# An encoder kernel on one core: moving the X, B and C projections ahead of the chunked scan as seven-product pairs

## The chip, the cores and the metric

The kernel runs on one core of a Trainium2 chip. The metric is the device time of one execution in microseconds (us). Engines are named as in the profile: PE (TensorE) with its weight loads PEld, DVE (VectorE), ACT (ScalarE), POOL (GpSimd) and SP (SyncE), which issues the transfers.

## What is computed

Two encoder layers run over 1024 tokens of width 1024. Only the first, the even one, is touched:

```python
proj = x @ w_in
z, xbc, dt_raw, sc_bg, sc_cg, sc_h, sc_gate = _split(proj, EVEN_SIZES)
xbc = jax.nn.silu(_depthwise_conv(xbc, conv_w, SSD_CONV_PAD) + conv_b)
xs, bm, cm = _split(xbc, (SSD_INNER, SSD_GROUPS * SSD_STATE, SSD_GROUPS * SSD_STATE))
y_a = _ssd_bidirectional(
...
y_a = _rms_norm(y_a.reshape(b, S, SSD_INNER).astype(x.dtype) * jax.nn.silu(z), norm_g)
y_b = sc_bg * _depthwise_conv(sc_cg * sc_h, sc_conv_w, (1, 1)) * jax.nn.silu(sc_gate)
return jnp.concatenate([y_a, y_b], axis=-1) @ w_out
```

So `x @ w_in` gives, in blocks of 128 channels, 8 blocks of X, 4 of B, 4 of C (each with a four-tap convolution over the tokens and a SiLU) and 4 x 8 blocks of the gated short convolution ("gate blocks"), beside z and dt. The scan (SSD) works on four groups of heads; a group g needs X blocks 2g and 2g+1, B block g and C block g.

## The kernel before, in words

All matmuls keep float32 accuracy by splitting each operand into a high and a low part (`split`, L481: ACT makes the high part, L483, and DVE or POOL the low one, L484) and multiplying three times (`mm3`, `mm6`, L401 to L412). The four tiles of x (high and low) stay in SBUF all through the first layer. They sit in the pool `big` of eight buffers of 2 MB; the other four serve in turn.

**A full block** (`op_fm`, L657) is one block of 128 output channels against all of x: eight steps kk of six matmuls of 512 columns into a PSUM tile `gps`. `fm_finish` (L617) then takes it out: for X, B and C a convolution and a SiLU by halves (`conv_half`, L585: an Identity on ACT, three scalar_tensor_tensor on DVE at L593, a Tanh on ACT, one more on DVE at L598) into the group's tile `xfm`; for gate blocks (`br_conv`, L603, and L637 to L653) products with a three-tap convolution, stored to DRAM as `ybd`.

**A pair** (`op_sp`, L891, with its weight sums in `op_sw`, L835) makes two blocks at once from 2 x 2 blocks by Winograd's scheme: seven block products of twelve matmuls of 512 columns each, where two full blocks would take eight. It needs four tiles of sums of x, `xT4` (`op_tp`, L821, also from `big`: two loads `xtraw` into the weight buffers `wraw`, four differences on DVE at L827, two splits). The raw weights of a pair (`sraw`, L841) use the same three `wraw` buffers. Pairs are used for the gate blocks j = 4 to 7: eight pairs, all behind the SSD.

**The SSD** per group: `op_p2` and `op_p2s` (L697, L717) for eight chunks: transposes of xfm into `xps`, scaling by DVE (L712), a split with POOL, the chunk's state `sps`; `op_z` (L677) adds the z projection of the chunk for groups 1 to 3 (24 matmuls of 256 columns); `op_p2b` (L745) ends the state recurrence. Then `op_p3f` and `op_p3b` (L756, L776) for eight chunks: a 512 KB row broadcast `E` loaded from DRAM, a mask added by DVE (L768; held behind the sixth chunk's L712 by an order edge), eight exponentials on ACT (L771), products on PE (`cbp`, `yo`, `yd`), sums on DVE and POOL, a gate on POOL (L798) and a store. A group's `xfm`, `zx` and `hin` come from `big`, so with the next group's xfm all eight buffers are taken.

**Order.** `main_plan` (L78) lists all steps: steps of full blocks stand in a queue and are pulled between the SSD's (F2 per chunk in the first half of a group, F3 in the second). Here they are the X, B, C blocks of group 0 (before the SSD) and of groups 1 to 3, and the gate blocks j = 0 to 3; 16 steps are left and run behind the SSD, beside `op_end`, the last two `op_tp` and the first pair's weight sums. The list is not the order of issue: the program is built with a scheduler that plans on a timeline, takes on each engine the earliest listed instruction that is ready in its plan, and gives buffers out of a pool as they are freed. `issue_after` adds an order edge. Weights come through `Weights` (L250): loads into three `wraw` buffers, splits into three `whi` and three `wlo`.

## Time and profile before

| | |
|---|---|
| median of 3 runs | 1423.87 us (1423.72 to 1426.09) |
| time of the profiled execution | 1426.95 us |
| its span in the profile | 1424.8 us |
| mean granted TensorE clock | 0.997 of full speed |
| start until the first full block, 0 to 35 us | PE busy 28.28 us |
| full blocks, z and SSD | 35 to 555 us |
| eight pairs behind the SSD, with the end of the first layer's gating | 555 to 727 us |
| output projection, second layer | 727 to 1425 us |

A line of the timeline or of the chain gives start, duration, engine, line of the kernel, operation, output tile <- inputs, shapes and count; in brackets the idle time ahead of it and who ended it. [...] Busy times of PE overlap: a matmul of 512 columns counts as 0.39 us, but the next starts 0.23 us after it.

### The profile page before, as it was taken

The numbers are of one execution on the slowest core, as the hardware profiler recorded it, in microseconds if no ns is written. First come the engines' busy times: TensorE is split into PE (matmuls) and PEld (weight loads), VectorE is DVE, ScalarE is ACT, GpSimd is POOL, SyncE is SP. The second block draws the span as 40 slices with busy tenths as digits, with TensorE's granted clock in tenths as the row PEclk, the third lists the DMA queues.
The fourth block names the chain that finished last, engine by engine and source line by source line (L and its number), as shares of the span: only waits on it lengthen the run. The fifth ranks groups of instructions, "written<-read, shape, count | busy, mean of one in ns | idle before, by whom it ended". The sixth has DMA issues, their size and how long they took to land.

```text
span 1424.8 us, 19565 instructions
## 1 busy us (share of the span) xinstructions
PE 1394.6 (98%) x7287; PEld 1187.2 (83%) x7287; DVE 931.3 (65%) x1512; ACT 655.7 (46%) x1301; POOL 478.7 (34%) x443
## 2 busy tenths in 40 slices
PE   8999999999999999999999999999999999999997
PEld 8887798888889787788888888898888888988886
DVE  5758858839965947866564543733327888888485
ACT  5446545537536423433243422522225888878410
POOL 0013635423733543433210430612310445546210
PEclk9999999999999999999999999999999999999999
DMA  7221523421430524232268355211100000001232
GB/s 253 69 72 45 119 75 91 109 82 32 144 114 10 150 82 140 80 95 74 85 196 274 104 159 192 81 32 45 44 23 1 1 1 1 1 31 60 89 118 89
DMA packets 47726, 123.39 MB, mean 87 GB/s; under 512 B 5512, under 2 KB 10384, under 8 KB 47632
## 3 DMA queue, kind: packets, MB, share of 16 engines
q1 hardware_dynamic: 47632, 122.14, 27.8%
q8 instruction: 58, 0.95, 0.3%
q14 instruction: 36, 0.29, 0.1%
HBM read 105.21 MB, written 16.91 MB: 86 GB/s over the span
## 4 chain that ended last, share of the span: by engine, by line
PE 79%; DVE 10%; DMA 3%; ACT 3%; issue 2%; POOL 2%; DVEq 0%; SPq 0%; ACTq 0%; POOLq 0%
PE sA L907 6%; PE gps L409 5%; PE gps L410 5%; PE gps L412 5%; PE ops L412 4%; PE ops L410 4%; PE ops L409 4%; PE tps L1390 3%; PE fps L404 3%; PE fps L402 3%; PE fps L403 3%; PE sD L907 3%; PE sps L402 2%; PE sps L403 2%; PE sps L404 2%
## 5 line engine op out<-in xcount | busy, mean ns | idle before, releaser
L409 PE MATMUL gps<-x,whi 128*128 128x512 f32 x512 | 206.2, 403 | 3.6 <-DVE cacc L593 3.0
L410 PE MATMUL gps<-x,whi 128*128 128x512 f32 x512 | 202.3, 395 | 0.0
L412 PE MATMUL gps<-x,wlo 128*128 128x512 f32 x512 | 162.8, 396 | 0.1
L484 DVE TENSOR_TENSOR wlo<-wraw,whi 128x1024 fp32r<-128x1024 f32 x66 | 85.4, 1297 | 76.7 <-ACT whi L483 76.5
L483 ACT CAST whi<-wraw 128x1024 fp32r<-128x1024 f32 x66 | 69.0, 1049 | 122.7 <-PE ops L412 38.6
L409 PEld LDWEIGHTS gps<-x,whi 128*128 128x128 f32 x512 | 96.7, 189 | 26.4 <-issue 3.1
L412 PEld LDWEIGHTS gps<-x,wlo 128*128 128x128 f32 x512 | 95.7, 189 | 21.2 <-issue 1.2
L410 PEld LDWEIGHTS gps<-x,whi 128*128 128x128 f32 x512 | 96.7, 189 | 19.7 <-issue 1.2
L1376 POOL TENSOR_SCALAR pt<-pt,sm 128x1024 f32<-128x1024 f32 x64 | 72.8, 1138 | 114.3 <-DVE sm L1375 63.3
L484 POOL TENSOR_TENSOR xdl<-xd,xdh 128x512 fp32r<-128x512 f32 (+1 forms) x32 | 40.2, 1256 | 178.7 <-ACT xdh L483 175.3
L484 DVE TENSOR_TENSOR PT<-tps,PT 128x512 fp32r<-128x512 f32 x128 | 84.1, 682 | 14.2 <-ACT PT L483 14.0
L771 ACT ACTIVATE E<-E,eb 128x128 f32<-128x128 f32 x256 | 78.4, 391 | 25.3 <-DVE E L768 17.9
L1370 DVE TENSOR_REDUCE nm<-sps 128x1 f32<-128x1024 f32 x64 | 77.9, 1218 | 9.5 <-PE sps L404 9.3
L987 POOL TENSOR_TENSOR rs<-rs,neghalf 128x1 f32<-128x1 f32 x16 | 12.9, 811 | 210.5 <-DVE nm L1022 142.8
L1374 ACT ACTIVATE pt<-sps,nm 128x1024 f32<-128x1024 f32 x64 | 71.8, 1122 | 17.4 <-DVE nm L1371 12.6
L483 ACT CAST PT<-tps 128x512 fp32r<-128x512 f32 x128 | 70.0, 588 | 17.2 <-PE tps L1390 16.6
L795 POOL TENSOR_TENSOR ta<-to,ta 128x256 f32<-128x256 f32 x56 | 57.5, 1027 | 53.0 <-DVE to L788 50.1
L402 PE MATMUL fps<-x1hi,whi 128*128 128x512 f32 x192 | 74.9, 390 | 0.0
L404 PE MATMUL fps<-x1hi,wlo 128*128 128x512 f32 x192 | 74.7, 389 | 0.0
L403 PE MATMUL fps<-x1lo,whi 128*128 128x512 f32 x192 | 74.7, 389 | 0.0
L593 DVE SCALAR_TENSOR_TENSOR cacc<-gps,vec,cacc 128x512 f32<-128x512 f32 (+1 forms) x96 | 71.5, 745 | 2.4 <-ACT cacc L589 1.4
L1390 PE MATMUL tps<-consts,pt 128*128 128x128 f32 x512 | 70.9, 274 | 0.6 <-DVE PT L484 0.3
(372 smaller groups left out, 3823.9 us busy)
## 6 DMA issues: line engine op xcount, KB each, us to landing
wraw<-in_wt_dram SPq DMA_DIRECT2D x82, 512.0 KB, 4.3
E<-crow SPq DMA_DIRECT2D x32, 512.0 KB, 5.6
sraw<-in_wt_dram SPq DMA_DIRECT2D x16, 512.0 KB, 4.3
yad<-yg SPq DMA_DIRECT2D x32, 128.0 KB, 2.2
ybd<-bra SPq DMA_DIRECT2D x16, 256.0 KB, 2.4
xtraw<-in_xT_dram SPq DMA_DIRECT2D x8, 512.0 KB, 3.8
yab<-yad SPq DMA_DIRECT2D x8, 512.0 KB, 3.5
ybr<-ybd SPq DMA_DIRECT2D x8, 512.0 KB, 4.4
```

The source lines that it names most:

```text
L402: nc.tensor.matmul(out, shi, mhi, start=start, stop=False)
L403: nc.tensor.matmul(out, shi, mlo, start=False, stop=False)
L404: nc.tensor.matmul(out, slo, mhi, start=False, stop=stop)
L409: nc.tensor.matmul(out, shi, mhi, start=start, stop=False)
L410: nc.tensor.matmul(out, shi, mlo, start=False, stop=False)
L412: nc.tensor.matmul(out, slo, mhi, start=False, stop=stop)
L483: nc.scalar.copy(out=hi, in_=src)
L484: lo_eng.tensor_tensor(out=lo, in0=src, in1=hi.bitcast(F32), op=ALU.subtract)
L771: A.activation(out=E4[:, d, h], in_=E4[:, d, h], func=AF.Exp, bias=eb4[:, c, d, 4 * g + h:4 * g + h + 1])
L907: PE.matmul(ps, s_[:, kk, :], x_, start=fresh and kk == 0 and m == 0, stop=kk == 3 and m == 2, skip_group_check=True)
L1370: V.tensor_reduce(out=nm, in_=ps, axis=AX.X, op=ALU.max)
L1390: PE.transpose(out=ps[:, P * c:P * c + P], in_=pt[:, P * (4 * h + c):P * (4 * h + c) + P], identity=k.ident)
```

## The change

- The first block of gates, j = 0, is computed as full blocks right after the z and dt projection. The four `op_tp` run beside it.
- X, B and C of all groups then run as eight pairs (one pair of B and C and one of X per group). Their convolution is on whole rows of 1024 out of SBUF (`conv_silu`), with a Silu on ACT in place of Tanh and a DVE multiplication, and the result goes to DRAM (`xbd`, 512 KB a block). Each group loads its 2 MB `xfm` back (`op_xl`), group 0 before the SSD, the next ones at the end of the first half of the group before.
- group 0's z goes to DRAM and back (`z0d`). The decay tables (`dt_chain`) are made ahead of the pairs, with buffers of the front pool `fp`.
- In the SSD the only full blocks are gates j = 1 to 4, 128 steps: 16 before group 0, 2 with each chunk of its first half, 3 with each chunk of every second half. In the second halves a block's first step has an order edge behind the group's last transpose (`op_hold`).
- The `big` tiles of the sums are given up for the SSD, so `op_tp` runs again as before: two in the last group's second half, two behind it. The queue of full blocks is empty by then.
- Six gate pairs (j = 5 to 7) stay behind the SSD.
- In the front pairs all three split weights of a pair take the three `whi`/`wlo` buffers; behind the SSD the third has buffers of its own, as before.

```diff
-F2, F3, FB, FC = 0, 6, 4, 0
-J0 = 4
+F2, F3, FB, FX = (2, 0, 0, 0), 3, 0, 16
+JF, J0 = 1, 5
...
-    def to_front(keys):
-        n = 0
-        while n < len(queue) and queue[n][2] != 0:
-            n += 1
-        queue[n:n] = [s for key in keys for s in tile_steps(key)]
-
...
-    for key in (("B", 0), ("C", 0), ("X", 0), ("X", 1)):
-        queue += tile_steps(key)
-    ops.append(("dt",))
-    pull(len(queue))
-    for j in range(J0):
+    def pairs(first, count, sched, final):
+        for n in range(first, first + count):
+            for i in range(7):
+                ops.append(("sp", n, i))
+                if n + 1 < first + count:
+                    ops.extend(("sw", n + 1, m) for m in sched.get(i, ()))
+            if n + 2 < first + count:
+                ops.append(("sw", n + 2, 0))
+            ops.extend(final.get(n, ()))
+
+    for j in range(JF):
         for q in BR_ORDER:
             queue += tile_steps(("br", q, j))
+    ops.append(("zx",))
+    per = len(queue) // 4
+    for t in range(4):
+        pull(per // 2)
+        ops.append(("tp", t))
+        if t == 3:
+            ops.append(("sw", 0, 0))
+        pull(per - per // 2)
+    pull(len(queue))
+    ops += [("sw", 0, i) for i in range(1, SW_N)]
+    ops.append(("sw", 1, 0))
+    ops.append(("dt",))
+    pairs(0, NF, SW_FRONT, {})
+    for j in range(JF, J0):
+        for q in BR_ORDER:
+            queue += tile_steps(("br", q, j))
+    ops.append(("ssd",))
+    pull(FX)
     for g in range(G):
         ops.append(("z0", g))
         pull(FB)
...
-            pull(F2)
+            pull(F2[g])
...
         if g + 1 < G:
-            to_front([("X", 2 * g + 2), ("X", 2 * g + 3), ("B", g + 1), ("C", g + 1)])
+            ops.append(("xl", g + 1))
+        ops.append(("hold", g))
         ops.append(("p3f", g, C3[0]))
-        pull(FC)
...
             pull(F3)
             ops.append(("p3b", g, c))
-        while any(s[1][0] in ("B", "C", "X") for s in queue):
-            pull(1)
+        ops.append(("hold", None))
...
-    ops += [("sw", 0, i) for i in range(SW_N)]
+    ops += [("sw", NF, i) for i in range(SW_N)]
     pull(len(queue))
-    ops.append(("sw", 1, 0))
-    for n in range(NP):
-        for i in range(7):
-            ops.append(("sp", n, i))
-            if n + 1 < NP and 0 < i + 1 < SW_N:
-                ops.append(("sw", n + 1, i + 1))
-        if n + 2 < NP:
-            ops.append(("sw", n + 2, 0))
-        if n in YA_P:
-            ops.append(("ya", YA_P.index(n)))
+    ops.append(("sw", NF + 1, 0))
+    pairs(NF, NP - NF, SW_BACK, {NF + n: [("ya", i)] for i, n in enumerate(YA_P)})
...
+SW_FRONT = {1: (1,), 3: (2,), 5: (3, 4), 6: (5,)}
+SW_BACK = {i: (i + 1,) for i in range(5)}
 SW_N = 6
 YA_P = (1, 2)
-PAIRS = [p for j in range(J0, 8) for p in ((("br", 1, j), ("br", 2, j)), (("br", 3, j), ("br", 0, j)))]
+PAIRS = [p for g in range(G) for p in ((("B", g), ("C", g)), (("X", 2 * g), ("X", 2 * g + 1)))]
+NF = len(PAIRS)
+PAIRS += [p for j in range(J0, 8) for p in ((("br", 1, j), ("br", 2, j)), (("br", 3, j), ("br", 0, j)))]
 NP = len(PAIRS)
...
-        self.limit = self.seq.index(("O", 0))
+        self.limits = [4 * JF, self.seq.index(("O", 0)), len(self.seq)]
+        self.limit = self.limits.pop(0)
...
     def release(self):
-        self.limit = len(self.seq)
-        self.split(self.used + 1 + self.ahead)
+        self.limit = self.limits.pop(0)
+        self.split(self.used + 1)
...
+    k.xbd = k.dram.tile([G, P, 4, S], F32, name="xbd")
+    k.z0d = k.dram.tile([P, NB, 256], F32, name="z0d")
...
+    def op_zx():
+        nonlocal fp
...
+            zs = view(dtp.tile([P, 512], F32, name="z0", tag="z0", bufs=2)[:, 0:256 * n], n)
...
+            nc.sync.dma_start(out=k.z0d[:, c:c + n], in_=zs)
...
+    def acc4(name):
+        return fp.tile([P, S], F32, name=name, tag="acc", bufs=2)
+
+    def op_dt():
+        tm = [view(acc4("dtmp"), 4) for _ in range(2)]
+        dt_chain(k, [t[:, i] for t in tm for i in range(4)], t4("rowT"), dtx)
+
+    def op_ssd():
+        nonlocal fp, cvp, tp, eb4, dw4, ecs4, et4
+        fctx.close()
+        fp = None
+        cvp = bctx.enter_context(tc.tile_pool(name="cvp", bufs=1))
+        tp = sctx.enter_context(tc.tile_pool(name="ssdt", bufs=1, side="right"))
         eb4, dw4, ecs4, et4 = (t.rearrange("p (c d h) -> p c d h", c=NB, d=2) for t in (k.eb, k.dw, k.ecs, k.etot))
+        op_xl(0)
+
+    def op_xl(g):
+        groups[g]["xfm"] = view(big(k, "xfm").bitcast(F32), 4)
+        for j in (2, 3, 0, 1):
+            nc.sync.dma_start(out=groups[g]["xfm"][:, j], in_=k.xbd[g, :, j])
 
...
+    def conv_silu(key, u):
+        kd = key[0]
+        g, j = (key[1] // 2, key[1] % 2) if kd == "X" else (key[1], 2 + "BC".index(kd))
+        idx = key[1] if kd == "X" else 8 + 4 * (j - 2) + g
+        w = lambda i: k.vec[:, V_CONVW + 4 * idx + i:V_CONVW + 4 * idx + i + 1]
+        acc = acc4("cacc")
+        A.activation(out=acc, in_=u, func=AF.Identity, bias=k.vec[:, V_CONVB + idx:V_CONVB + idx + 1], scale=w(2))
+        for i, sh in ((1, -1), (0, -2), (3, 1)):
+            a0, a1 = max(-sh, 0), S - max(sh, 0)
+            V.scalar_tensor_tensor(out=acc[:, a0:a1], in0=u[:, a0 + sh:a1 + sh], scalar=w(i), in1=acc[:, a0:a1], op0=ALU.mult, op1=ALU.add)
+        A.activation(out=acc, in_=acc, func=AF.Silu)
+        nc.sync.dma_start(out=k.xbd[g, :, j], in_=acc)
...
+    hold = None
+
+    def op_hold(g):
+        nonlocal hold
+        hold = None if g is None else groups[g]["xp"]
 
     def op_fm(key, kk):
         if kk == 0:
             live[key] = (W.get(key), k.pa.tile([P, 1024], F32, name="gps", tag="pa"))
         (whi, wlo), ps = live[key]
         wh, wl = view(whi, KD), view(wlo, KD)
-        mm6(nc, halves(ps), wh[:, kk, :], wl[:, kk, :], *zip(*(xhl(h, kk) for h in range(2))), kk == 0, kk == KD - 1)
+        with tc.issue_after(hold) if hold is not None and kk == 0 else nullcontext():
+            mm6(nc, halves(ps), wh[:, kk, :], wl[:, kk, :], *zip(*(xhl(h, kk) for h in range(2))), kk == 0, kk == KD - 1)
...
     def op_z0(g):
         st = groups[g]
+        zx = big(k, "zx").bitcast(F32)
+        st["zs"], st["xtm"] = view(zx[:, 0:2048], NB), view(zx[:, 2048:4096], NB)
         if g > 0:
             st["zw"] = (W.get(("Z", g, 0)), W.get(("Z", g, 1)))
-            zx = big(k, "zx").bitcast(F32)
-            st["zs"], st["xtm"] = view(zx[:, 0:2048], NB), view(zx[:, 2048:4096], NB)
+        else:
+            nc.sync.dma_start(out=st["zs"], in_=k.z0d)
...
-            st["S2"], st["S4"] = wsplit(k.w2, (("b4h", 2), ("b4l", 2)), r1)
+            st["S2"], st["S4"] = wsplit(W.pool, (("whi", 3), ("wlo", 3)), r1) if n < NF else wsplit(k.w2, (("b4h", 2), ("b4l", 2)), r1)
...
+        lo, hi = slice(0, HALF), slice(HALF, S)
+        if n < NF:
+            if i == 0:
+                st["p1"] = snap(ps)
+            elif i == 1:
+                st["u1"] = t4("u1")
+                comb(st["u1"][:, lo], ps, st.pop("p1"))
+                if n == NF - 1:
+                    W.release()
+            elif i == 2:
+                st["v"] = snap(ps)
+            elif i == 3:
+                st["d7"] = snap(ps)
+            elif i == 4:
+                st["u2"] = t4("u2")
+                comb(st["u2"][:, hi], ps, st.pop("d7"))
+            elif i == 5:
+                comb(st["u2"][:, lo], ps, st.pop("v"))
+                conv_silu(PAIRS[n][1], st.pop("u2"))
+            else:
+                A.copy(out=st["u1"][:, hi], in_=ps)
+                conv_silu(PAIRS[n][0], st.pop("u1"))
+            return
```

## Rows read from the trace of the kernel before

**Rows 1.** The page, busy time, share and instructions of each engine.

```profile
PE 1394.6 (98%) x7287; PEld 1187.2 (83%) x7287; DVE 931.3 (65%) x1512; ACT 655.7 (46%) x1301; POOL 478.7 (34%) x443
```

**Rows 2.** The chain that ended last, two products of a pair behind the SSD.

```profile
661.90 2.72 PE sA L907 x12
664.62 2.72 PE sD L907 x12
```

**Rows 3.** The page, costliest groups: full block matmuls; weight splits; convolution taps.

```profile
L409 PE MATMUL gps<-x,whi 128*128 128x512 f32 x512 | 206.2, 403 | 3.6 <-DVE cacc L593 3.0
L484 DVE TENSOR_TENSOR wlo<-wraw,whi 128x1024 fp32r<-128x1024 f32 x66 | 85.4, 1297 | 76.7 <-ACT whi L483 76.5
L593 DVE SCALAR_TENSOR_TENSOR cacc<-gps,vec,cacc 128x512 f32<-128x512 f32 (+1 forms) x96 | 71.5, 745 | 2.4 <-ACT cacc L589 1.4
```

**Rows 4.** Stages: group 0's second half; the pairs behind the SSD.

```profile
134.00:181.00 47.00, 45.05 (x226) 35.77 (x225) 43.01 (x64) 22.78 (x59) 31.00 (x34) 1.00 0.52 110
575.00:727.00 152.00, 151.61 (x699) 125.79 (x700) 100.85 (x104) 54.09 (x73) 48.17 (x32) 1.00 0.28 91
```

**Rows 5.** Timeline of PE, from the last SSD products to the first pair.

```profile
532.07 0.59 PE L785 MATMUL yo<-hin,xfm 128*128 128x256 f32 x2
532.50 1.00 PE L791 MATMUL yd<-zx,E 128*128 128x64 f32 x8
533.30 0.48 PE L409 MATMUL gps<-x,whi 128*128 128x512 f32 x1
555.33 0.62 PE L907 MATMUL sA<-x,whi 128*128 128x512 f32 x2
```

**Rows 6.** Timeline of SP in the same stretch.

```profile
538.25 6.10 SPq L824 DMA_DIRECT2D xtraw<-in_xT_dram  x2
546.97 0.34 SPq L841 DMA_DIRECT2D sraw<-in_wt_dram  x1
```

**Rows 7.** Timeline of DVE in the same stretch.

```profile
537.13 1.89 DVE L614 SCALAR_TENSOR_TENSOR bra<-bru,vec,bra 128x511 f32<-128x511 f32 x2
544.53 1.28 DVE L645 TENSOR_TENSOR bra<-gps,bra 128x512 f32<-128x512 f32 x2
552.21 1.22 DVE L484 TENSOR_TENSOR wlo<-sraw,whi 128x1024 fp32r<-128x1024 f32 x1
```

**Rows 8.** The page, DMA issues: half-megabyte loads and stores.

```profile
E<-crow SPq DMA_DIRECT2D x32, 512.0 KB, 5.6
xtraw<-in_xT_dram SPq DMA_DIRECT2D x8, 512.0 KB, 3.8
```

**Rows 9.** Timeline of PE in group 0's first half.

```profile
121.85 0.62 PE L409 MATMUL gps<-x,whi 128*128 128x512 f32 x1 [2.15 <-DVE cacc L593]
```

**Rows 10.** Stages: the two stretches around that wait.

```profile
119.00:122.10 3.10, 0.95 (x5) 0.49 (x4) 3.10 (x7) 3.10 (x12) 0.56 (x1) 1.00 0.00 0
122.10:125.50 3.40, 3.40 (x9) 2.65 (x9) 3.16 (x6) 3.40 (x7) 1.11 (x1) 0.50 0.02 5
```

**Rows 11.** Stages, full block matmuls only: first halves of groups 1 to 3; second of 0.

```profile
186.50:220.00 33.50, 8.98 (x34) 1.00 0.08 24
298.10:346.00 47.90, 23.29 (x96) 1.00 0.11 37
421.30:456.60 35.30, 10.68 (x42) 1.00 0.10 31
134.00:181.00 47.00, 33.53 (x127) 1.00 0.52 110
```

**Rows 12.** Timeline of DVE in group 1's first half.

```profile
208.36 6.13 DVE L768 TENSOR_TENSOR E<-E,consts 128x1024 f32<-128x1024 f32 x4
```

**Rows 13.** Groups of DVE by line in group 2's first half.

```profile
L614 DVE SCALAR_TENSOR_TENSOR bra<-bru,vec,bra 128x511 f32<-128x511 f32 (+1 forms) x4 | 3.9, 1000 | 0.0
L484 DVE TENSOR_TENSOR wlo<-wraw,whi 128x1024 fp32r<-128x1024 f32 x2 | 2.4, 1214 | 0.0
```

**Rows 14.** Groups of DVE by line, whole span: a 1024-wide sum.

```profile
L641 DVE TENSOR_TENSOR bru<-gps,bru 128x1024 f32<-128x1024 f32 x4 | 4.9, 1215 | 4.8 <-PE gps L412 4.8
```

More of the change, by code (lines that the diff above doesn't have):

```diff
@@ L1 @@
-from contextlib import ExitStack
+from contextlib import ExitStack, nullcontext
 import numpy as np
@@ L577, in cv @@
     def cv(name):
-        return cvp.tile([P, 512], F32, name=name, tag="cv", bufs=CVB)
+        return (fp or cvp).tile([P, 512], F32, name=name, tag="cv", bufs=2 if fp is not None else CVB)
     def t1(name, dt=F32):
@@ L617, in fm_finish @@
     def fm_finish(key, ps):
-        kd = key[0]
-        if kd == "X":
-            g, j = key[1] // 2, key[1] % 2
-            st = groups[g]
-            if j == 0 and "xfm" not in st:
-                st["xfm"] = view(big(k, "xfm").bitcast(F32), 4)
-            for h in range(2):
-                conv_half(ps, key[1], st["xfm"][:, j, HALF * h:HALF * h + HALF], h)
-        elif kd in ("B", "C"):
-            g, q = key[1], "BC".index(kd)
-            st = groups[g]
-            if "xfm" not in st:
-                st["xfm"] = view(big(k, "xfm").bitcast(F32), 4)
-            for h in range(2):
-                conv_half(ps, 8 + 4 * q + g, st["xfm"][:, 2 + q, HALF * h:HALF * h + HALF], h)
-        else:
-            q, j = key[1], key[2]
-            hs = [slice(0, HALF), slice(HALF, S)]
-            if q == 1:
-                br["u"] = t4("bru")
-                A.copy(out=br["u"], in_=ps)
-            elif q == 2:
-                u = br["u"]
-                V.tensor_tensor(out=u, in0=ps, in1=u, op=ALU.mult)
-                br_conv(u, j)
-            elif q == 0:
-                for h in range(2):
-                    V.tensor_tensor(out=br["a"][h], in0=ps[:, hs[h]], in1=br["a"][h], op=ALU.mult)
-            else:
-                for h in range(2):
-                    th = cv("brt")
-                    A.activation(out=th, in_=ps[:, hs[h]], func=AF.Tanh, scale=0.5)
-                    V.scalar_tensor_tensor(out=th, in0=th, scalar=1.0, in1=ps[:, hs[h]], op0=ALU.add, op1=ALU.mult)
-                    acc = br["a"][h]
-                    GP.tensor_tensor(out=acc, in0=acc, in1=th, op=ALU.mult)
-                    nc.sync.dma_start(out=k.ybd[j, :, hs[h]], in_=acc)
@@ new lines, in fm_finish @@
+        q, j = key[1], key[2]
+        hs = [slice(0, HALF), slice(HALF, S)]
+        if q == 1:
+            br["u"] = t4("bru")
+            A.copy(out=br["u"], in_=ps)
+        elif q == 2:
+            u = br["u"]
+            V.tensor_tensor(out=u, in0=ps, in1=u, op=ALU.mult)
+            br_conv(u, j)
+        elif q == 0:
+            for h in range(2):
+                V.tensor_tensor(out=br["a"][h], in0=ps[:, hs[h]], in1=br["a"][h], op=ALU.mult)
+        else:
+            for h in range(2):
+                th = cv("brt")
+                A.activation(out=th, in_=ps[:, hs[h]], func=AF.Tanh, scale=0.5)
+                V.scalar_tensor_tensor(out=th, in0=th, scalar=1.0, in1=ps[:, hs[h]], op0=ALU.add, op1=ALU.mult)
+                acc = br["a"][h]
+                GP.tensor_tensor(out=acc, in0=acc, in1=th, op=ALU.mult)
+                nc.sync.dma_start(out=k.ybd[j, :, hs[h]], in_=acc)
@@ L702, in op_p2 @@
         for j in range(3):
-            PE.transpose(out=ps[:, P * j:P * j + P], in_=st["xfm"][:, j, P * c:P * c + P], identity=k.ident)
+            st["xp"] = PE.transpose(out=ps[:, P * j:P * j + P], in_=st["xfm"][:, j, P * c:P * c + P], identity=k.ident).ins
         A.copy(out=st["xtm"][:, c, :], in_=ps[:, 0:256])
@@ L854, in op_sw @@
         elif i == 2:
-            t = k.w2.tile([P, HALF], F32, name="s3t", tag="s3t", bufs=1)
+            t = (fp or k.w2).tile([P, HALF], F32, name="s3t", tag="s3t", bufs=1)
             GP.tensor_tensor(out=t, in0=h1[0], in1=h2[0], op=ALU.subtract)
-            s3 = k.w2.tile([P, 2, HALF], F32R, name="s3", tag="s3", bufs=2)
+            s3 = (fp or k.w2).tile([P, 2, HALF], F32R, name="s3", tag="s3", bufs=1 if fp is not None else 2)
             split(nc, s3[:, 0], s3[:, 1], t, V)
@@ L945, in op_sp @@
             W.release()
+            W.split(W.used + 1 + W.ahead)
     k.ay = {}
@@ L960, in op_ya @@
         split(nc, t[:, 0, :, o:o + P], t[:, 1, :, o:o + P], view(y, KD), V)
[L962 removed]
+    table = {"fm": op_fm, "hold": op_hold, "zx": op_zx, "ssd": op_ssd, "xl": op_xl, "z0": op_z0, "z": op_z, "p2": op_p2, "p2s": op_p2s, "p2b": op_p2b, "p3f": op_p3f, "p3b": op_p3b, "dt": op_dt, "rope": lambda: rope_tables(k, t2), "end": op_end, "ya": op_ya, "tp": op_tp, "sw": op_sw, "sp": op_sp}
     for op in main_plan():
```

73 lines of the change are left out of this document (24 added, 49 removed).

## The prediction, made before the change was run

> **What bounds the kernel now.** I read the page's busy shares first: PE is busy for 98% of the span, the next engine, DVE, for 65% [rows 1]. Busy alone says little, since the ends of matmuls overlap, so I looked at the pace. In the chain of waits a block product of a pair, twelve matmuls of 512 columns, takes 2.72 us, product after product without a hole: 0.227 us a matmul [rows 2]. Full blocks run at the same pace, 48 matmuls or 10.9 us a block; the row of one of their three matmul lines counts 512, two for each of eight steps, so there are 32 blocks [rows 3]. From 35 to 555 us the holes in PE's timeline are few. The stages' table says why: in the second half of group 0 PE is busy for 45.05 of 47.00 us although DVE is busy for 43.01, and behind the SSD for 151.61 of 152.00 us [rows 4]. So every matmul that goes is worth its 0.227 us, as long as something stands ready for PE in its place. The full blocks are what stands ready: they need only x and a weight, and the plan lays them into every hole of the SSD. The change takes twelve of those 32 away.
>
> **The sum, part by part**, against the profiled execution's own 1426.95 us, 3.1 above the median of 1423.87; differences are carried over to the median.
>
> *Products.* Twelve X, B, C blocks net move from full blocks to pairs: full blocks go from 32 to 20, pairs from 8 to 14. A pair is 84 matmuls, two blocks 96. Six pairs more save 72 x 0.227 = **-16.3 us** [rows 2, 3]. This is certain.
>
> *The end of the SSD.* The sums of x for the pairs are made anew. Their last three tiles get a buffer only when the last yo product has read xfm and hin, at 532.07, and PE's own SSD work ends where the next full block begins, at 533.30 [rows 5]. From there runs a chain of splits and of loads through the three raw weight buffers: the last loads of x issue from 538.25 on, the first raw weight of a pair only at 546.97, when a buffer is given back [rows 6], and DVE ends its split at 552.21 + 1.22 = 553.43 [rows 7]. Before, 16 steps of full blocks, 21.8 us, lie over this chain and the first pair starts right behind them, at 555.33 [rows 5]. After, the queue is empty there. PE waits 553.43 - 533.30 = 20.1 us, less the gate convolution and product that leave DVE in the middle of the chain, 1.89 and 1.28 [rows 7]: **+16.9 us**. Lower bound 12: two loads of x or weights at 3.8 behind each other [rows 8] and three splits of 1.22; upper 20.1. What is late next is the pair's second raw weight, but two products, 5.4 us, need only the first.
>
> *The clock.* [...] I put one such stretch behind the long wait: **+1.7**. [...]
>
> *First halves of groups 1 to 3.* Here the plan now lays 34, 96 and 42 full-block matmuls between the first and the last transpose [rows 11], 172 x 0.227 = 39.0 us. They stand last in the list for these stretches, so each was taken because nothing else was ready. The change pulls none there and the new order edge keeps those of the second half behind the last transpose; in PE's queue they, and nothing of the first half, stand behind that edge. Upper bound 39.0 lost, lower 0, if z and transposes close up. The bound that lasts is DVE: after the sixth chunk four mask additions take it for 6.13 us in a row [rows 12], and the last chunks wait behind them. Three times 6.13 is 18.4; in group 2, where the rotary tables also run, 3.9 of gate convolution and 2.4 of weight splits leave DVE [rows 13]. I take 18.4 - 6.3 = **+12**.
>
> *Second halves.* 24 steps (32.6 us) are pulled in each. Group 0 ran just so before: 127 full-block matmuls, 28.8 us, within 47.00 us [rows 4, 11]. I take 0, from -3 to +9.
>
> *Group 0's first half.* There the 2.15 us wait was for a convolution tap on DVE [rows 9], and the clock fell behind it. The convolutions are gone from there: **-3.9** (2.15 + 1.7), from -3.9 to +5.
>
> *The front pairs.* Per pair DVE has three splits at 1.30 [rows 3], one of half size, five half-width sums at about 0.7 (two of them take 1.28 [rows 7]) and six taps of 1024. No row has such a tap from SBUF; twice the half-width 0.745 [rows 3] is 1.49, a plain 1024-wide sum takes 1.22 [rows 14]. I take 1.25, nearer to the one that has the same width. That is 15.5 us, at most 17, beside PE's 19.0. The SiLU multiplication leaves DVE. The six taps now wait for the pair's last two products, and the third split weight of the next pair (S2 and S4) can only be made when the last product has left its buffer. Behind the last product but one DVE has two convolutions (7.5), sums and two splits, about 10.8 us, before PE needs S2; PE has the seventh product, the next two and S3's to run meanwhile, 10.9. Just enough: **+3** for eight pairs, from 0 to 22.
>
> *Transfers and queues.* The stores to DRAM wait on SP for ACT's Silu, with the loads of the pair after next behind them, which have a pair's time of slack; the group loads (2 MB) run beside 16 full-block steps or a whole second half, at 3.8 a half megabyte [rows 8]; the mask rows of E behind them on SP have four buffers. z of group 0 is needed late. The decay tables run under the front blocks. I take 0, up to +5, if cover is gone at the SSD's start. POOL gets nothing new on the path.
>
> Sum: -16.3 + 16.9 + 1.7 + 12 - 3.9 + 3 = +13.4, so **1437 us**. That is slower by 0.9%.
>
> **Rivals.**
>
> *The SSD closes up and the end is short (faster).* With convolutions and twelve weight splits out of the SSD the first halves run dense, the wait at the end is at its lower bound and the second halves gain: -16.3 + 12 + 1.7 + 0 - 3.9 - 3 = -9.5, 1414 us. For it: DVE's 43.01 of 47.00 [rows 4], much of it convolution. Against: the mask additions stay.
>
> *Only the end is lost (no change).* First halves close, the end is as I have it: -16.3 + 16.9 + 1.7 - 3.9 + 3 = +1.4, 1425. It says that the wait at the end alone eats the products.
>
> *The front pairs run at DVE's pace (slower still).* If the plan does not pull S3's product ahead, S2 is late by about 10.8 - 8.2 + half a microsecond of handing over = 3.1 us at each of seven pair borders: +22 on top of my sum less its 3, 1456 us. It decides once DVE needs more than 19.0 us a pair.
>
> That the change does not do what it says would mean full blocks left over behind the SSD, since the list is not the order of issue; but PE takes listed steps as early as it can, and I give that no case of its own: it would end as the first rival.
>
> **How the numbers follow.** My case 0.49, the SSD that closes 0.27, only the end 0.13, DVE's pace 0.11. A measurement of this kernel can tell about 0.2%, 2.8 us, from no change. Faster is the first rival, 0.27; of the second, 0.11 lies within 0.2% and 0.02 above; with my case and the third that makes 0.62 slower. The range holds my case with its end between 12 and 20 and its first halves between 5 and 25, and reaches down to just under the first rival and up past the third: 1411 to 1462. My case alone spans 1425 to 1453.
>
> **What would show it.** Right: front pairs at 19.0 us each on PE; in PE's timeline one hole of 15 to 20 us behind the last yd, ended by the split of a pair's first raw weight, and behind it a stretch at half clock; holes of 3 to 6 us ahead of the last transpose of groups 1 to 3, ended by DVE. Wrong: full-block matmuls behind the last yo; first halves no longer than their own matmuls; front pairs over 20 us, with PE waiting for the third split weight; PE waiting for a group's xfm. If the page shows no hole at the end of the SSD, my largest term falls and the change is faster.

## The result, and the profile after

The changed kernel takes 1469.28 us (median of 4 runs, 1467.8 to 1471.3) against 1423.85 for the kernel before on the same chip: a ratio of 1.0313, 95% interval 1.0292 to 1.0333. That is slower, as predicted, but by 45 us where 13 were forecast, and outside the range. The profiled execution has a span of 1466.5 us, 41.7 over the span before.

First the page of the changed kernel: busy time and instructions [rows 1], and the granted clock in 40 slices.

```profile
PE 1394.8 (95%) x7215; PEld 1185.9 (81%) x7215; DVE 959.6 (65%) x1499; ACT 683.8 (47%) x1317; POOL 488.1 (33%) x452
PEclk9999999998998999879999999999999999999999
```

PE has 72 matmuls less, as counted, but fills 95% of its span instead of 98%. Several slices fall under 9, so time went both into holes and into a slower granted clock behind them, down to 0.50 in the last rows of the table of stages. Where it went, that table says. As in [rows 4], a line has the stretch, its length, busy time and instructions of PE, PEld, DVE, ACT and POOL, the granted clock as a share of the full one, the transfers' share and their GB/s; its boundaries are the ends and starts of stages in PE's timeline.

```profile
33.70:40.30 6.60, 0.32 (x3) 0.09 (x2) 5.62 (x13) 3.20 (x5) 0.00 (x0) 0.80 0.38 121
...
88.40:249.00 160.60, 160.60 (x707) 132.26 (x706) 124.13 (x119) 80.39 (x97) 29.86 (x16) 1.00 0.32 115
...
263.50:290.80 27.30, 27.30 (x135) 22.76 (x134) 20.62 (x29) 16.77 (x46) 10.17 (x10) 1.00 0.59 187
...
347.50:378.10 30.60, 28.56 (x211) 27.19 (x211) 16.46 (x31) 17.83 (x58) 14.85 (x17) 0.93 0.40 113
378.10:432.70 54.60, 53.29 (x273) 43.19 (x272) 33.43 (x53) 24.71 (x71) 33.92 (x39) 1.00 0.45 123
432.80:476.10 43.30, 31.86 (x212) 28.96 (x211) 34.58 (x81) 25.17 (x73) 13.21 (x14) 0.88 0.34 89
...
529.80:559.40 29.60, 27.04 (x211) 25.36 (x210) 17.95 (x33) 18.90 (x58) 13.28 (x14) 1.00 0.29 62
559.40:620.50 61.10, 55.26 (x273) 45.23 (x271) 48.73 (x74) 28.09 (x74) 36.39 (x35) 0.92 0.36 98
620.50:636.00 15.50, 0.54 (x4) 0.35 (x3) 11.49 (x13) 5.29 (x10) 11.12 (x10) 0.50 0.59 168
636.00:639.40 3.40, 3.40 (x9) 2.73 (x9) 1.64 (x2) 1.80 (x3) 2.36 (x2) 0.50 0.32 125
639.40:642.80 3.40, 3.40 (x11) 2.64 (x11) 3.37 (x5) 2.60 (x4) 0.00 (x0) 0.65 0.56 175
```

The first row is a hole in the start, with DVE busy for 5.62 of 6.60 us. The second is the front pairs, with some full-block matmuls among them: 707 matmuls in 160.60 us, 0.227 us each, not a hole in them. The third is the first half of group 0, without a hole too. The fourth, sixth and seventh rows are the first halves of groups 1, 2 and 3: the same 211 or 212 matmuls, but 43.30 us in group 2 against 30.60 and 29.60, and DVE busy for 34.58 us there against 16.46 and 17.95. The fifth and eighth rows are the second halves of groups 1 and 3: 273 matmuls each, in 54.60 and 61.10 us. The last three are the wait behind the SSD and the first pair behind it, at a granted clock of 0.50 and then 0.65.

The four longest holes that the kernel before does not have stand in PE's timeline, each with who ended it.

```profile
40.33 0.77 PE L423 MATMUL gps<-x,whi 128*128 128x512 f32 x1 [6.31 <-DVE dtx L571]
...
470.39 0.58 PE L416 MATMUL zps<-whi,x 128*128 128x256 f32 x1 [5.75 <-DVE hin L751]
...
614.81 0.80 PE L782 MATMUL cbp<-xfm 128*128 128x128 f32 x2 [5.84 <-DVE E L794]
...
635.85 0.38 PE L830 MATMUL rinvp<-consts,rinv 128*8 128x128 f32 x1 [14.96 <-DVE rinv L828]
635.95 1.19 PE L928 MATMUL sA<-x,whi 128*128 128x512 f32 x2
```

To set these beside the prediction I took, for every stage of both kernels, its length less what its matmuls take at the pace that their shape has when nothing waits (0.227 us for 512 columns, 0.119 for 256, some 0.10 for the small ones, 0.43 for a `yo` of 512), from the starts of all matmuls up to the first of the output projection, at 712.4 us before and 754.0 after. What is left over is time in which PE waited or ran below full clock:

| stage | left over before | after | change | predicted |
|---|---|---|---|---|
| products (72 matmuls) | | | -16.3 | -16.3 |
| start, z and dt, first gate blocks | 9.9 | 17.7 | +7.8 | 0 |
| front pairs, to the SSD | | 1.0 | +1.0 | +3 |
| group 0 | 7.8 | 7.8 | 0 | -3.9 |
| first halves, groups 1 / 2 / 3 | 0.5 / 0.6 / 0.5 | 4.9 / 17.6 / 3.9 | +24.8 | +12 |
| second halves, groups 1 / 2 / 3 | 1.1 / 1.7 / 1.5 | 3.0 / 2.1 / 9.6 | +10.4 | 0 |
| behind the SSD, with the pairs and the clock | 4.4 | 18.6 | +14.2 | +18.6 |

The changes add up to 41.9, the timeline has 41.6. From the output projection on, the two kernels run alike (712.4 and 712.5 us). Three lines carry the error: the start, group 2's first half, and group 3's second half.

### The profile page after: what moved, and what is told of

Read it like the earlier page. It is cut to its first block, busy times and chain, and to the rows that moved or that the text cites. A ratio compares the mean times of both kernels' runs of the same rounds, so it can differ in the third digit from the quotient of the medians.

```text
span 1466.5 us, 19571 instructions
## 1 busy us (share of the span) xinstructions
PE 1394.8 (95%) x7215; PEld 1185.9 (81%) x7215; DVE 959.6 (65%) x1499; ACT 683.8 (47%) x1317; POOL 488.1 (33%) x452
## 4 chain that ended last, share of the span: by engine, by line
PE 78%; DVE 8%; DMA 6%; POOL 3%; issue 2%; ACT 2%; SPq 0%; DVEq 0%; ACTq 0%; POOLq 0%
PE sA L928 11%; PE sD L928 5%; PE ops L423 4%; PE ops L424 3%; PE ops L426 3%; PE gps L423 3%; PE gps L424 3%; PE tps L1434 3%; PE gps L426 3%; PE fps L416 3%; PE fps L418 3%; PE fps L417 3%; PE sB L928 3%; PE sps L416 2%; PE sps L417 2%
## 5 line engine op out<-in xcount | busy, mean ns | idle before, releaser
L423 PE MATMUL gps<-x,whi 128*128 128x512 f32 x320 | 130.5, 408 | 6.3 <-DVE dtx L571 6.3
L424 PE MATMUL gps<-x,whi 128*128 128x512 f32 x320 | 128.9, 403 | 0.0
L493 DVE TENSOR_TENSOR wlo<-wraw,whi 128x1024 fp32r<-128x1024 f32 x54 | 69.1, 1279 | 70.3 <-ACT whi L492 70.1
L492 ACT CAST whi<-wraw 128x1024 fp32r<-128x1024 f32 x54 | 56.6, 1048 | 113.8 <-PE ops L426 44.5
L426 PE MATMUL gps<-x,wlo 128*128 128x512 f32 x320 | 103.3, 400 | 0.0
L792 ACT ACTIVATE E<-E,dtx 128x128 f32<-128x128 f32 x256 | 79.1, 392 | 39.1 <-DVE E L789 32.9
L877 POOL TENSOR_TENSOR s3t<-sraw 128x512 f32<-128x512 f32 x14 | 24.2, 1731 | 216.3 <-DMA sraw<-in_wt_dram 163.3
L493 DVE TENSOR_TENSOR PT<-tps,PT 128x512 fp32r<-128x512 f32 x128 | 84.2, 682 | 13.6 <-ACT PT L492 13.4
L1418 ACT ACTIVATE pt<-sps,nm 128x1024 f32<-128x1024 f32 x64 | 71.8, 1122 | 17.1 <-DVE nm L1415 13.4
L423 PEld LDWEIGHTS gps<-x,whi 128*128 128x128 f32 x320 | 60.7, 190 | 21.1 <-issue 9.9
L424 PEld LDWEIGHTS gps<-x,whi 128*128 128x128 f32 x320 | 60.8, 190 | 14.1 <-issue 2.6
L426 PEld LDWEIGHTS gps<-x,wlo 128*128 128x128 f32 x320 | 60.2, 189 | 13.7 <-issue 1.4
L626 DVE SCALAR_TENSOR_TENSOR cacc<-u,vec,cacc 128x1023 f32<-128x1023 f32 (+1 forms) x48 | 66.8, 1408 | 1.5 <-ACT cacc L623 1.3
```

What stands on the lines that cost most here:

```text
L423: nc.tensor.matmul(out, shi, mhi, start=start, stop=False)
L424: nc.tensor.matmul(out, shi, mlo, start=False, stop=False)
L426: nc.tensor.matmul(out, slo, mhi, start=False, stop=stop)
L492: nc.scalar.copy(out=hi, in_=src)
L493: lo_eng.tensor_tensor(out=lo, in0=src, in1=hi.bitcast(F32), op=ALU.subtract)
L792: A.activation(out=E4[:, d, h], in_=E4[:, d, h], func=AF.Exp, bias=eb4[:, c, d, 4 * g + h:4 * g + h + 1])
```

## The experiments

Theory A was that each stage loses what its own chain on DVE, ACT and POOL is longer than the matmuls listed there, so that each loss is local and full blocks (or any work that waits for nothing) cover it where they lie. Theory B was that DVE as a whole is the bound, so that a loss moved away comes back elsewhere. Theory C was that the order edge, which keeps full blocks out of the first halves, is the cause. Each run is given by its ratio to the kernel before on its own chip; a difference of 0.0021 between two ratios is 3 us, and the intervals are about 0.002 to either side, so differences of that size are settled by the stages and not by the totals. "Lost" in the expectations counts delays matmul by matmul, which gives some 2 us more for a second half than the table above.

**The rotary tables, moved to group 0.**

```diff
-ROPE_AT = (2, 2)
+ROPE_AT = (0, 0)
```

> The rotary tables are listed in the first half of group 0, where 16 steps of full blocks lie, and no longer in group 2's. Theory A (each stage loses what its own chain on DVE needs beyond the work listed for PE): group 2's first half shrinks from 43.4 us between first and last transpose to about 31, as in groups 1 and 3 (30.7 and 29.7), group 0's grows by at most 3; in all -10 to -13 us, 1456 to 1459. Theory B (DVE as a whole is the bound of the SSD, so moved work costs the same elsewhere): what group 2 gains, group 0 loses, within 4 us of 1469. Theory C (the order edge that keeps full blocks out of the first halves is the cause, whatever DVE does): group 2 keeps a loss of over 10 us.

Ratio 1.0292 (1.0273 to 1.0311), 3 us less. The stages of this run: group 0's first half, group 2's; then PE's waits in the former (who waits for whom, us in all, times, longest).

```profile
263.80:302.00 38.20, 30.66 (x138) 24.04 (x137) 35.12 (x76) 21.18 (x57) 15.76 (x12) 0.89 0.49 155
...
445.00:476.60 31.60, 27.79 (x212) 25.63 (x212) 21.39 (x37) 19.74 (x60) 13.26 (x14) 1.00 0.47 121
```

```profile
PE sps L417 <- POOL xdl L493: 6.5, 3, 3.8
```

Group 2 shrinks from 43.30 to 31.60 us, so the tables were the loss there, 11.7 us of it, and theory C falls for it. But group 0 grows from 27.30 to 38.20 us. It has 96 full-block matmuls, yet they ran ahead as soon as they could, and the holes came behind them, between 289.9 and 300.6 us. So theory A's forecast of the total was missed, and the total by itself is what theory B expected; the next run parts the two. Cover in the same stage is not enough: it has to lie where the wait is.

**The rotary tables, listed among the front pairs.**

```diff
-    pairs(0, NF, SW_FRONT, {})
+    pairs(0, NF, SW_FRONT, {2: [("rope",)]})
...
-            if (g, i) == ROPE_AT:
-                ops.append(("rope",))
...
-"rope": lambda: rope_tables(k, t2)
+"rope": lambda: rope_tables(k, lambda nm: fp.tile([P, P], F32, name=nm, tag="rp", bufs=8))
```

> The rotary tables are made beside the front pairs (with small buffers of their own), where PE has 19 us of products a pair that wait for no hand-over but the weights, and DVE about 3.5 us a pair to spare. Theory A (work on DVE costs what lies on a chain that PE has nothing else to do beside; beside the front pairs it has): group 2's first half 43.3 to about 31 us, the front pairs grow by at most 2 us, in all -9 to -12 us, 1457 to 1460. Theory B (DVE as a whole is the bound, so it costs the same wherever it is): the front pairs grow by 8 us or more, as group 0's first half did by 10, and the sum stays within 4 us of 1469. The rival of the prediction that the front pairs stand close to DVE's pace says the same as B.

Ratio 1.0242 (1.0223 to 1.0261), 10 us less. The stages: front pairs, and group 2's first half.

```profile
91.10:252.30 161.20, 160.93 (x708) 132.21 (x706) 127.96 (x131) 84.69 (x102) 28.17 (x15) 1.00 0.32 115
436.10:467.40 31.30, 27.96 (x211) 25.80 (x211) 21.50 (x37) 19.88 (x61) 14.06 (x14) 0.98 0.46 122
```

The total is in theory A's range, but the tables did not run where the expectation puts them. They were listed behind the third pair and taken earlier, where DVE was free. These are their first instruction on DVE, one shortly before the first pair begins at 91.1 us, and their last.

```profile
56.08 0.23 DVE L362 TENSOR_TENSOR ang<-posf,invf 128x128 f32<-128x128 f32 x1
...
90.12 1.31 DVE L399 TENSOR_TENSOR racc<-racc,ang 128x128 f32<-128x128 f32 x1
...
98.89 0.34 DVE L409 COPY cos<-cos 128x128 f32<-128x128 f32 x1 [0.91 <-ACT cos L408]
```

Of these 43 small instructions 33 began beside the full blocks ahead of the pairs and 10 in the first 8 us of the pairs. What they cost there is some 3 us: the pairs begin at 91.1 us, where the changed kernel and the five runs with the same start have 88.4 to 89.1, and they take 161.20 us in place of 160.60. In either group they cost 11 us. So theory B falls: work moved on DVE did not come back in full. The rival that the front pairs stand at DVE's pace is hardly tried by this run, since DVE has only 3.8 us more in the pairs; the changed kernel's own row speaks against it, 160.60 us without a hole while DVE is busy for 124.13.

**Without the order edge.**

```diff
-        hold = None if g is None else groups[g]["xp"]
+        hold = None
```

> The order edge of the full blocks behind a group's last transpose is gone; by the issue order the first halves of groups 1 to 3 then take 17, 89 and 17 full-block matmuls and the last group's second half has none. Theory A: a full block in a hole earns what the hole was worth, so the first halves get back 10 to 20 of their 25.7 us lost, but the last group's second half stands without cover and loses 20 to 35 us in place of 11: in all 0 to +20 us, 1469 to 1490. Theory C (the edge itself is what costs): -10 us or more, 1459 or less.

Ratio 1.035 (1.0327 to 1.0373), 5 us more. Here are group 2's first half, with 89 full-block matmuls in it, and group 3's second half, with none:

```profile
439.20:485.80 46.60, 46.60 (x301) 42.16 (x301) 34.09 (x80) 24.15 (x68) 16.72 (x16) 1.00 0.36 108
580.40:626.70 46.30, 33.10 (x129) 24.09 (x126) 32.06 (x52) 20.05 (x62) 27.13 (x33) 0.69 0.32 83
```

The first is dense, tables or not. The second shows the bare length of such a half: 46.30 us for 18.9 us of matmuls at full pace, 27 us of room. The order edge is no cost; it saves blocks for the halves that need them more.

**A fourth step a chunk in the second halves**, with 32 steps taken back from two pairs.

```diff
-F2, F3, FB, FX = (2, 0, 0, 0), 3, 0, 16
-JF, J0 = 1, 5
+F2, F3, FB, FX = (2, 0, 0, 0), 4, 0, 16
+JF, J0 = 1, 6
```

> Gate blocks j = 5 are full blocks again (32 more steps, two pairs fewer), all put into the second halves: four steps a chunk where there were three. The products cost 24 x 0.227 = 5.4 us. Theory A (a second half loses what its own chain is longer than the listed matmuls): its 48 matmuls more, 10.9 us, lie mostly in holes, so the four second halves, 8.4 + 5.2 + 4.0 + 11.3 = 28.9 us lost, fall to 10 to 14; net -10 to -13 us, 1456 to 1459. Rival (the holes come from instructions that wait in a fixed order, a row of E behind a store on SP, and stay whatever is listed): the loss stays above 22 us, 1468 to 1475.

Ratio 1.0196 (1.018 to 1.0213), 17 us less although the products cost 5.4 more. The second halves of groups 1 and 3:

```profile
381.00:444.00 63.00, 63.00 (x321) 51.94 (x320) 40.33 (x60) 27.79 (x76) 30.81 (x38) 1.00 0.43 115
...
579.60:644.50 64.90, 63.86 (x320) 51.78 (x319) 48.77 (x70) 28.99 (x78) 34.99 (x38) 1.00 0.39 102
```

Group 3's half takes 48 matmuls more (10.9 us) in 3.8 us more; group 1's is now without a hole. This is theory A's side, and beyond the range that I gave it.

**Steps kept for the end.**

```diff
-F2, F3, FB, FX = (2, 0, 0, 0), 3, 0, 16
+F2, F3, FB, FX = (0, 0, 0, 0), 3, 0, 16
```

> The 16 steps that stood in group 0's first half stay in the queue to the end; 90 full-block matmuls then stand behind the last yd. Theory A (the 15.3 us behind the SSD are the chain to the first pair's weights, uncovered): the hole behind the last yd closes to under 2 us, the half clock behind it goes, the last group's second half is as before; group 0's first half, uncovered now, loses about what groups 1 and 3 lose there, 4 to 5 us: in all -9 to -13 us, 1456 to 1460. Rival (what ends the hole is the transpose of rinv ahead of the first product, which comes late whatever stands before it): the hole stays above 5 us, and the sum is within 4 us of 1469.

Ratio 1.0289 (1.0264 to 1.0313), 3 us less. Group 0's first half, and the stretch from the last yd to the first pair:

```profile
263.90:284.70 20.80, 11.80 (x42) 8.32 (x41) 17.43 (x27) 15.41 (x43) 9.80 (x10) 0.67 0.91 220
...
607.40:630.00 22.60, 20.99 (x95) 16.96 (x94) 18.05 (x25) 9.47 (x15) 6.76 (x6) 1.00 0.41 134
```

The hole at the end closes (1.9 us left over), though the pairs behind it then lose some 6 us where they lost 3. Group 0 pays 15, not the 4 to 5 that I expected, and the total misses its range: unlike the other groups it has no z products in its first half, so with the blocks gone PE has 5.7 us of work in 20.80.

**The kernel before, with the cover at its end moved to the starts of the groups.**

```diff
-F2, F3, FB, FC = 0, 6, 4, 0
+F2, F3, FB, FC = 0, 6, 8, 0
```

> The kernel before, with one number changed: 16 more steps are pulled at the starts of the groups, so that none is left behind the SSD (96 full-block matmuls stood there). If the wait for the first pair's weights behind the SSD is 15 us by itself and only covered in the kernel before: a hole of 13 to 18 us behind the last yd, and since the other stages of that kernel lose too little to take the steps up (about 17 us in all four groups, of which 3 may come back), +9 to +15 us, 1432 to 1438. If the hole belongs to the change (its other order of weights and buffers): hole under 5 us, within 4 us of the kernel before.

Ratio 1.0138 (1.0118 to 1.0158), 20 us more, above my range. PE behind the last yd, which ends at 561.0:

```profile
572.43 0.37 PE L809 MATMUL rinvp<-consts,rinv 128*8 128x128 f32 x1 [11.16 <-DVE rinv L807]
574.61 1.22 PE L907 MATMUL sA<-x,whi 128*128 128x512 f32 x2 [1.81 <-ACT whi L483]
```

One number makes a hole of 13.6 us in the old kernel that is like the one of the changed kernel. The wait is not the change's own; the 16 steps of [rows 5] hid it.

**The transpose of the inverse norms, behind the third product** of the first pair (`rinv` a step of its own).

```diff
+                if (n, i) == (NF, 2):
+                    ops.append(("rinv",))
```

> Only the row of inverse norms of the gating (rinv: DVE, a power on POOL, a transpose on PE) is listed behind the first back pairs' third product, where it stood ahead of the first one in PE's queue. In the changed kernel the first pair's split ends at 632.4 and PE began at 635.9, behind that transpose. Theory A (the hole is the chain loads, differences, splits; the transpose adds its own wait at the end): the hole shrinks from 15.3 to 11 to 13 us, ended by the split of the first raw weight, -2.5 to -4 us, about 1466. Rival (the transpose is what the hole is made of): the hole shrinks to under 6 us, -9 us or more. Rival (the wait only moves to the next instruction in line): within 1.5 us of 1469.

Ratio 1.031 (1.0291 to 1.0329): no change. The wait is shorter, but a new one further on gave most of the time back:

```profile
621.20:630.80 9.60, 0.44 (x3) 0.25 (x2) 7.08 (x8) 3.82 (x8) 8.45 (x8) 0.50 0.61 193
630.80:641.00 10.20, 9.90 (x32) 7.22 (x33) 6.41 (x10) 4.40 (x7) 5.45 (x4) 0.74 0.38 116
...
653.00:657.00 4.00, 3.87 (x10) 3.12 (x11) 2.94 (x3) 2.00 (x4) 0.00 (x0) 0.57 0.43 131
```

```profile
653.13 1.22 PE L932 MATMUL sA<-xT,whi 128*128 128x512 f32 x2 [2.22 <-ACT snap L896]
```

The hole falls from 15.5 to 9.6 us, since the first two products need only the high part of the weight to begin. Then 32 matmuls take 10.2 us where 7.3 would do, but the changed kernel loses as much behind its hole (2.9 us, by its clocks of 0.50 and 0.65). What it does not have is the hole of 2.22 us at 653.13, where PE waits for ACT, and the clock of 0.57 behind it: together with short waits at the next weights they take back some 4.5 us. The last rival holds: the wait moved on.

**The start: the differences behind z.** In the changed kernel DVE stood like this in the start (timeline of DVE):

```profile
34.61 2.15 DVE L848 TENSOR_TENSOR xtraw<-xtraw 128x512 f32<-128x512 f32 x3 [1.88 <-DMA xtraw<-in_xT_dram]
36.67 1.22 DVE L493 TENSOR_TENSOR xT<-xtraw,xT 128x1024 fp32r<-128x1024 f32 x1
37.81 0.45 DVE L571 TENSOR_TENSOR dtx<-zdp,dtb 128x64 f32<-128x64 f32 x3
```

The first differences for the sums of x wait for their load and stand ahead of the dt and z evictions, which hold the PSUM buffer that the first full block needs; PE waited 6.31 us, up to the last of the dt evictions (L571). An order edge turns that round:

```diff
+            with tc.issue_after(k.zlast):
+                V.tensor_tensor(out=o, in0=p, in1=q, op=ALU.subtract)
```

> The differences for the sums of x get an order edge on DVE behind the last z eviction of group 0; nothing else is changed. Theory A (in the start DVE stood with these differences, waiting for a load, ahead of the dt and z evictions that free the PSUM buffer of the first full block): the hole of 6.5 us at 33.7 us shrinks to about 1, the first full block starts near 35 us as in the kernel before, and the whole is 4 to 6 us shorter, 1463 to 1465. Rival (the pairs ahead of the SSD then wait for the sums made later): the first pair starts no earlier than 88 us and the time stays within 1.5 us of 1469.

Ratio 1.0292 (1.027 to 1.0314), 3 us less. The first block starts at 34.3, but a hole of the same size opens further on:

```profile
85.19 1.89 PE L485 MATMUL rps<-consts,cs 128*32 128x128 f32 x8 [6.27 <-ACT cs L471]
```

These transposes of the decay tables stand ahead of the first pair's products. Two runs moved them. In the first, all of the decay tables came behind the first pair (`{0: [("dt",)]}`):

> As in the run with the order edge in the start, and the decay tables are listed behind the first front pair, so that their transposes no longer stand ahead of that pair's products in PE's queue (there they took over the hole, 6.5 us at 78.5). Theory A (in-order waits, each removable): both holes gone, the first pair starts at 80 to 82 us in place of 88.4, in all -6 to -8 us, 1461 to 1463. Theory B (the start is bound by DVE, busy 37 of 48 us there): the pair starts at 85 or later, waiting for its weights or sums of x, and the sum is within 4 us of 1469.

Ratio 1.0431 (1.041 to 1.0451), 17 us more. The first pair did start at 79.2, but the tables share two buffers with the convolutions, and their matmuls now held up the second pair:

```profile
120.97 0.80 PE L462 MATMUL cps<-dtmp,consts 128*128 128x128 f32 x2 [20.87 <-DVE dtmp L456]
```

In the second only the part with matmuls was moved, behind the first pair's second product:

```diff
+                if (n, i) == (0, 1):
+                    ops.append(("dt2",))
```

> The order edge in the start again, and the decay tables stay where they were, except that their PE part (cumulative sums, transposes) is listed behind the first pair's second product. In the run with the edge alone 6.5 us of hole went over to these transposes; in the run with all tables behind the first pair PE waited 20.9 us for them, since they shared buffers with the convolutions. Theory A (waits in a fixed order, each removable): lost time before the pairs falls from 10.9 to about 3 us, the first pair starts at 79 to 81 us and the pairs stay at 160 to 163 us: -6 to -9 us, 1460 to 1463. Theory B (DVE-bound start): the hole comes back at a third place, in the first pair, and the sum stays within 4 us of 1469.

Ratio 1.0283 (1.0265 to 1.0302), 4 us less. The profiled execution is the fastest of the four, so its stages show somewhat more than that. The stages from the first block on, and the hole that is left:

```profile
34.10:77.60 43.50, 43.50 (x194) 35.99 (x193) 34.69 (x58) 14.35 (x18) 0.00 (x0) 1.00 0.38 126
77.60:242.90 165.30, 162.45 (x719) 133.65 (x718) 128.35 (x125) 84.20 (x104) 34.20 (x18) 1.00 0.34 120
```

```profile
86.93 0.73 PE L934 MATMUL sA<-xT,whi 128*128 128x512 f32 x2 [2.85 <-ACT snap L898]
```

Two waits in a fixed order made the loss, and each could be taken out; some 3 us came back at a third place, which is part of what theory B expected.

**All that helped, together.** Gate blocks 5 and 6 as full blocks, steps `(2, 1, 1, 0), 4, 0, 16`, 16 behind the SSD; and the same without the steps in groups 1 and 2, 32 behind the SSD.

> All that helped, together, with more full blocks: gate blocks j = 5 and 6 are full blocks again (64 steps, four pairs fewer, 2 x 5.4 us of products back, so 5.4 less than the kernel before), four steps a chunk in second halves, one a chunk in the first halves of groups 1 and 2, 16 behind the SSD; rotary tables beside the front pairs; the start as in the run beside this one. If each loss is local and covered as the single runs say, 25 us are lost up to the output projection where the kernel before loses 27: 1416 us, 1412 to 1424, the same as or just under the kernel before. If losses come back elsewhere (a DVE bound): 1430 or more.

> As the run of all that helped, but without steps in the first halves of groups 1 and 2: those 16 stand behind the SSD too, 32 in all, where about 10 would cover the chain. If a step is worth only what hole it lies in: these two first halves lose about 4.5 us each in place of 1, the end gains nothing more, so 5 to 8 us over that run. If any cover is as good as any other: within 2 us of it.

Ratios 1.0063 (1.0047 to 1.0078) and 1.0108 (1.009 to 1.0127). Neither beats the kernel before; the first is 36 us below the changed kernel. It missed the 1412 to 1424 us that it was to take if each loss were local, and lies where losses that come back elsewhere were to put it, at 1430 or more. Its stages: front pairs, group 1's first half, the end, the two pairs left with the gating up to the output projection.

```profile
79.20:248.60 169.40, 165.41 (x718) 135.04 (x719) 137.19 (x140) 88.77 (x109) 35.42 (x18) 0.98 0.33 117
351.50:388.70 37.20, 37.20 (x259) 34.40 (x259) 20.16 (x35) 19.38 (x62) 15.26 (x14) 1.00 0.31 104
...
650.30:672.40 22.10, 22.10 (x100) 18.23 (x100) 18.26 (x26) 8.57 (x12) 5.32 (x3) 1.00 0.45 140
672.40:722.20 49.80, 43.55 (x202) 35.32 (x201) 34.18 (x34) 19.67 (x25) 15.83 (x11) 0.98 0.38 125
```

The SSD is nearly closed. What keeps it over the kernel before is the front, where tables and decay tables together now cost 8 us, and the gating at the end, which has two pairs to lie beside instead of eight (8.5 us). The second run is 6 us over the first. There eight steps less in a first half cost it 2.5 us (3.1 us left over in group 1 against 0.6). The 16 steps more behind the SSD, beyond what covers the chain, ran among the last two pairs and closed the waits of the first run there, some 3 us; so they earned something, but less than in the two first halves. The rest of the 6 us is not told apart from the spread of the runs (1437 to 1444 us). Cover is worth the hole that it lies in.

## Why the prediction was right and wrong

**Products**, -16.3: right, 72 matmuls.

**The end of the SSD**, +16.9 and +1.7 for the clock: right in place and, by some luck, in size. The hole is 15.5 us, 1.4 under the estimate; what was lost behind it is 3.1 and not 1.7, since the granted clock was 0.50 for 3.40 us and then 0.65 for as long again. The two errors cancel to the 18.6 us forecast. It came to 14.2 net, because the pairs behind the SSD already lost 4.4 us in the kernel before, 3 of it in three holes from 564 to 575 us. The cause was right for 9.6 us of the hole. The step overlooked the transpose that stands ahead of the first product, on which the other 5.9 hang; moving it changed the hole and not the sum.

**Front pairs**, +3: right. The stretch lost 1.0 us. DVE is busy for 124.13 us, 15.5 a pair, as added up, though the stretch holds only 45 of the 48 taps and a tap took 1.41 us and not 1.25, near the upper bound. The third rival (1456 us, for this reason) was wrong even though its time was nearer. No row and no run shows the half microsecond of handing over in its sum; at the waits of PE in the kernel before, from 35 to 712 us, PE begins 0.04 to 0.15 us after the instruction that releases it. The first two rivals both needed first halves that close up, and those lost 26.4 us.

**Group 0**, -3.9 and 0: the 2.15 us wait of [rows 9] went, but its second half lost as much anew.

**First halves of groups 1 to 3**, +12: this step failed, in one of its three terms. Groups 1 and 3 lost 4.9 and 3.9, somewhat less than the 6.13 us of mask additions [rows 12] that I priced for each. For group 2 I wrote that the rotary tables also run there, took off 6.3 us for gate convolution and weight splits that leave DVE [rows 13], and put no price on the tables themselves. They are some 13 us of DVE: without them, in the run that moved them to group 0, DVE is busy for 21.39 us in this stretch in place of 34.58. The 6.3 us, too, did not leave as assumed: most of the rest of the 18 us by which DVE is busier there than in group 1 (34.58 less 16.46) is a gate block's end and a weight split, still in that stretch.

```profile
L643 DVE SCALAR_TENSOR_TENSOR bra<-bru,vec,bra 128x511 f32<-128x511 f32 (+1 forms) x4 | 3.4, 868 | 0.0
...
L493 DVE TENSOR_TENSOR wlo<-wraw,whi 128x1024 fp32r<-128x1024 f32 x1 | 1.2, 1225 | 0.9 <-ACT whi L492 0.9
L654 DVE TENSOR_TENSOR bru<-gps,bru 128x1024 f32<-128x1024 f32 x1 | 1.2, 1216 | 0.0
```

The tables are what cost: taking them out gave 11.7 us back (the first run) and 12.0 (the second), and group 2 then lost 5.9 and 5.6 us, little more than the others. The rows before told it: group 2 took 96 full-block matmuls where groups 1 and 3 took 34 and 42 [rows 11]. If each was taken because nothing else was ready, the 58 more than the mean of the other two, 58 x 0.227 = 13.2 us, are an estimate of the tables' price, and a near one. The upper bound of the step, 39, held.

**Second halves**, 0: this failed for group 3 alone, +8.1 of the +10.4. I compared with group 0's second half; but group 3's also makes two tiles of sums of x on DVE, busy there for 48.73 us. Ahead of its longest hole stand these rows, two of SP and one of DVE:

```profile
597.80 5.90 SPq L821 DMA_DIRECT2D yad<-yg  x2
603.81 0.38 SPq L786 DMA_DIRECT2D E<-crow  x1
...
610.56 1.23 DVE L789 TENSOR_TENSOR E<-E,consts 128x1024 f32<-128x1024 f32 x1 [2.87 <-DMA E<-crow]
```

The load of the row E stood behind a store on SP that waited for the gate, so it was issued at 603.81, and DVE waited 2.87 us for it. That the store delayed it is read from the trace and was not tried by itself. One step more a chunk covered most of the loss (64.90 us with 48 matmuls more, against 61.10).

**Start**, 0 in "transfers and queues": this failed too, +7.8. The moved step `op_tp` was priced in its transfers and not in its place on DVE: I never asked what it passes there. It passed the evictions of z and dt, and behind that wait stood a second one, the decay tables' transposes.

**The clock.** The +1.7 is half of the 3.40 us that [rows 10] show at a granted clock of 0.50, behind the wait of 2.15 us of [rows 9]. In the changed kernel the clock was 0.50 behind the two longest holes inside the SSD too: from 470.5 to 474.0 us behind the one of 5.75, and from 614.8 to 618.2 behind the one of 5.84. Over a whole half it was 0.88 in group 2's first, 0.92 in group 3's second and 0.93 in group 1's first. For the first halves I had priced no slow clock; two of the three had one, and the third, group 3's, stayed at 1.00.

So the frame of the prediction held: full blocks were the cover, and the change spends it. The sum failed because two of the places that they covered, and one step that moved, carried no price: 13, 8 and 8 us, about the 28.5 us by which the sum was short (41.9 less 13.4).

## What to carry to other kernels

Before filler is removed, read what it covers stage by stage: how much the planner laid in a stretch, against a like stretch, is the price of what is hidden there, work that looks free included. Then list, for every step that moves, which instructions it passes on each engine's queue. Filler is worth the hole that it lies in and nothing beyond, so a kernel with little of it wants it portioned out by the bare length of each stage; and work on another engine cost least here beside long runs of matmuls that wait for nothing (the rotary tables some 3 us, against 11 in a group). Where a step is listed is not yet where it runs: look it up in the trace before a run is read as a test of the place.

## What was unexpected

The rotary tables cost 11 us in either of two groups and some 3 us beside the first full blocks and the first pair, the same instructions. A wait that was cut by 5.9 us gave next to nothing, since a new one of 2.22 us opened 22 us later, with a granted clock of 0.57 behind it. And without any full block a second half, with its many waits of 0.5 to 2.5 us, ran at a mean granted clock of 0.69 over 46.30 us: there short waits too, and not only holes of 5 us and more, went with a slow clock.
